# Score products of a two-block transformer kernel, all contracted over 96 or 128 rows

## The chip, the cores and the metric

The kernel runs on one core of a Trainium2 chip. The metric is the device time of one execution in microseconds (us); lower is better. TensorE (PE) does the matrix products, its weight loads have a row of their own in the profile (PEld), VectorE (DVE), ScalarE (ACT) and GpSimd (POOL) do the elementwise work, and DMA transfers are issued from SyncE's queue (SP) and from POOL's.

## The reference, cut to what matters

Two blocks of two layers each work on 512 tokens of width 1024, everything in float32. In the first block each of 8 query heads of 64 columns, sharing 2 key heads, attends to 256 context tokens and to a window around its own 128 tokens; the context's queries attend to the context alone:

```python
s_loc = jnp.einsum('bqkgd,bnkd->bkgqn', qi, ks).astype(jnp.float32)
s_ctx = jnp.einsum('bqkgd,bnkd->bkgqn', qi, kc).astype(jnp.float32)
p = sink_softmax(jnp.concatenate([s_ctx, s_loc], axis=-1), sink_b).astype(v.dtype)
```

The second block has 16 heads of three kinds: 6 of kind A (mixtures of dilated windows, 64 columns), 4 of kind B (the difference of two softmaxes, each over 32 columns), and 6 of kind C (latent, 64 + 32 columns). All of them are causal:

```python
a = probs(q1, k1) - lam * probs(q2, k2)          # kind B
s = jnp.einsum('bqhd,bkhd->bhqk', qs, k)         # kind C
```

Both blocks go on with an output projection and norms, the second also with a gated feed-forward of width 2816. A modulation of the first block's layers comes from two vectors c and c_ctx.

## The kernel before

Every float32 operand of a large product is held as the sum of a high and a low part of a narrower kind (fp32r). `split` (line 175) makes them: `hi` on ACT writes the high part, `lo` on DVE subtracts it. `mm3` (line 208) then adds three products: high by high, high by low, low by high. Weights arrive on SP's queue in chunks of 512 KB and are split the same way (`w`, line 179).

The program is written as a sequence of steps. A scheduler orders them by their place in the text and by what they wait for, within the limits of the named buffers, and each engine then works through its own fixed queue. `high_priority(offset=n)` moves what stands inside ahead by n instructions. PSUM, where products land, is divided into three buffers `acc`, two score buffers `s` (`sps`), two for transposes (`tp`) and one for attention outputs (`pv`).

*First block's attention* (`first_mix`, `first_att`). The keys of both heads lie in KS as their high part, on both halves of the 128 rows, and in KTl as their low part, on the 64 rows of their own head. The queries Q hold the high part on 64 rows and the low part on the other 64. So one product over 128 rows (lines 819 and 825) gives high by high and low by high at once, and one over 64 rows (lines 820 and 826) adds high by low:

```python
nc.tensor.matmul(p1[:, kc], Q[:, g, hq, :], KS[:, g, kc], start=True, stop=False)
nc.tensor.matmul(p1[:, kc], Q[r, g, hq, :], KTl[r, kc], start=False, stop=True)
```

Between them stand the products of the next queries, of transposes and values, and of gate blocks (`tblock`). Layer 0 has 6 query tiles of 128 tokens (2 of them context), layer 1 has 4.

*Second block's attention* (`second_mix`, `att2`). Heads come in pairs, in the order of UNITS (line 34), here A B C B C A C A. `proj(i + 1)` projects the next pair's queries, keys and values (`proj_t`, 24 products of 512 columns each for kinds A and B) and splits them; then `att` of pair i follows, moved ahead by AHEAD = 102 instructions. `direct` (line 1113) leaves a pair of kind A or B in four tiles of 128 rows, qh, ql, kh, kl (`pair`, 8 buffers of the tag qk, line 1005); a head of kind A is 64 rows of them, one softmax of kind B 32 rows. `att2` makes three products for each of 4 query tiles:

```python
for k, (x, y) in enumerate(((0, 2), (0, 3), (1, 2))):
    for ps, s in zip(pss, subs):
        nc.tensor.matmul(ps[:, :w], s[x][:, tok], s[y][:, :w], start=(k == 0), stop=(k == 2))
```

The four tiles have w = 256, 256, 384 and 512 columns. For kind B, `subs` holds both softmaxes, so their products alternate. Line 1025 (DVE) then adds the distance table T, which POOL's queue loads for each head (line 947, two buffers), and takes the extreme; line 1029 (ACT) takes the exponential; line 1048 or 1050 (DVE) divides or combines; line 1060 transposes, lines 1063 to 1069 split, lines 1074 to 1077 multiply by the values. Kind C has queries and keys of 128 rows of its own and the same three products. `fin` of kind B norms the pair's output with a tile sq, kind C's projection uses a tile qu, and `vpair` a tile vt.

*Modulation* (`mod_rows`, `mod_later`). A product gives rows of which four are used, copied by line 324 into a tile of 5 rows; line 369 contracts over these 4 rows, line 395 over 5.

## Time and profile before

| | us |
|---|---|
| median of 3 runs | 2070.19 (2068.41 to 2079.08) |
| span of the profiled execution, first to last instruction | 2059.4 |
| PE busy in it | 2006.9 (97%) |
| DVE busy | 1204.4 (58%) |
| ACT busy | 877.2 (43%) |
| POOL busy | 123.1 (6%) |

The profiled execution has no time of its own beside its span; between the span and the median of the runs lie 10.8 us. The granted TensorE clock is 0.993 of full speed on average. An instruction's row gives its engine, the line of the kernel, the tiles that it writes and reads, and its shape: `64*128 64x256` is a product that contracts 64 rows, with 128 columns of weights and 256 columns streamed. Products are pipelined, so that one starts before the end of the one before it; the distance from start to start is what one costs. Idle time stands in brackets with what ended it.

### The profile page before, as it was taken

Reading aid. Unit: us, or ns where it says so; the run is one execution under the profiler, and the core shown is the slowest. Engines: PE = TensorE matmul, PEld = TensorE weight load, DVE = VectorE, ACT = ScalarE, POOL = GpSimd, SP = SyncE. Lnnn points to the kernel's source line nnn. Section 1 sums busy time; section 2 is a strip of 40 time slices with the busy share of each in tenths; the row PEclk is TensorE's granted clock in tenths of the full one; section 3 lists DMA queues with packets and bytes.
Section 4 is the critical chain, followed back from the end, with each engine's and each line's share of the span. In section 5 each row is a group of like instructions: output and inputs, shape, how many; then the busy total and the mean of one; then the engine's idle time right before and its main releaser. Section 6 shows DMA issues by size and latency. Waiting matters only on the chain. (4 is left out here: it accounts for less than half of the span.)

```text
span 2059.4 us, 25829 instructions
## 1 busy us (share of the span) xinstructions
PE 2006.9 (97%) x9692; PEld 1584.7 (77%) x9692; DVE 1204.4 (58%) x2386; ACT 877.2 (43%) x1708; POOL 123.1 (6%) x230
## 2 busy tenths in 40 slices
PE   6999999999999999999999999999999999999997
PEld 4877778778776786767788888888677788888886
DVE  3758875366787575777643333346677664333434
ACT  4736553376455444656332222214566523222220
POOL 2000000021000020000100000011000010000001
PEclk9999999999999999999999999999999999999999
DMA  8413433134331163212342323316112333332321
GB/s 287 149 37 93 123 103 93 42 103 127 93 92 51 52 184 88 56 47 83 103 133 82 107 88 100 101 61 162 46 47 62 118 103 113 92 98 76 113 82 41
DMA packets 220448, 197.19 MB, mean 96 GB/s; under 512 B 30154, under 2 KB 178128, under 8 KB 220324
## 3 DMA queue, kind: packets, MB, share of 16 engines
q1 hardware_dynamic: 209940, 160.32, 26.8%
q0 software_dynamic: 10384, 35.24, 5.0%
q8 instruction: 76, 1.25, 0.3%
q14 instruction: 48, 0.39, 0.1%
HBM read 187.09 MB, written 12.03 MB: 97 GB/s over the span
## 5 line engine op out<-in xcount | busy, mean ns | idle before, releaser
L165 ACT ACTIVATE wh<-wr 128x1024 fp32r<-128x1024 f32 (+3 forms) x299 | 311.6, 1044 | 645.0 <-PE acc L213 304.6
L169 DVE TENSOR_TENSOR wl<-wr,wh 128x1024 fp32r<-128x1024 f32 (+3 forms) x299 | 358.5, 1202 | 268.6 <-ACT wh L165 267.8
L212 PE MATMUL acc<-xt,wh 128*128 128x512 f32 (+1 forms) x1200 | 470.3, 392 | 0.0
L213 PE MATMUL acc<-xt,wh 128*128 128x512 f32 (+1 forms) x1200 | 469.1, 391 | 0.0
L214 PE MATMUL acc<-xt,wl 128*128 128x512 f32 (+1 forms) x1200 | 468.3, 390 | 0.0
L213 PEld LDWEIGHTS acc<-xt,wh 128*128 128x128 f32 x1200 | 227.2, 189 | 47.1 <-issue 3.8
L212 PEld LDWEIGHTS acc<-xt,wh 128*128 128x128 f32 x1200 | 226.6, 189 | 47.4 <-issue 3.2
L214 PEld LDWEIGHTS acc<-xt,wl 128*128 128x128 f32 x1200 | 226.7, 189 | 45.1 <-issue 1.8
L212 PE MATMUL acc<-wh,ht 128*128 128x512 f32 (+1 forms) x494 | 192.6, 390 | 0.0
L213 PE MATMUL acc<-wl,ht 128*128 128x512 f32 (+1 forms) x494 | 191.9, 388 | 0.0
L214 PE MATMUL acc<-wh,ht 128*128 128x512 f32 (+1 forms) x494 | 191.5, 388 | 0.0
L165 ACT ACTIVATE pth<-tps 128x384 fp32r<-128x384 f32 (+1 forms) x176 | 90.9, 537 | 101.0 <-PE tps L789 50.6
L169 DVE TENSOR_TENSOR ptl<-tps,pth 128x384 fp32r<-128x384 f32 (+1 forms) x176 | 105.0, 614 | 43.5 <-ACT pth L165 39.7
L1029 ACT ACTIVATE L<-L,nm 128x128 f32<-128x128 f32 (+3 forms) x160 | 89.2, 558 | 49.2 <-DVE nm L1025 47.7
L214 PEld LDWEIGHTS acc<-wh,ht 128*128 128x128 f32 x494 | 92.8, 188 | 21.6 <-DVE ht L169 0.9
L212 PEld LDWEIGHTS acc<-wh,ht 128*128 128x128 f32 x494 | 92.8, 188 | 20.6
L213 PEld LDWEIGHTS acc<-wl,ht 128*128 128x128 f32 x494 | 92.8, 188 | 20.1
L1025 DVE CUSTOM_DVE_ANT_0 L<-sps,T 128x128 f32<-128x128 f32 (+3 forms) x160 | 76.3, 487 | 46.9 <-PE sps L1022 45.7
L1400 DVE SCALAR_TENSOR_TENSOR h<-h,acc 128x512 f32<-128x512 f32 (+1 forms) x50 | 33.2, 665 | 114.6 <-PE acc L214 114.6
L1366 DVE SCALAR_TENSOR_TENSOR th<-th,acc 128x512 f32<-128x512 f32 x42 | 28.9, 688 | 112.1 <-PE acc L214 111.9
L214 PE MATMUL acc<-wh,xt 128*128 128x256 f32 (+2 forms) x256 | 85.5, 335 | 1.1 <-DVE xt L169 0.8
L212 PE MATMUL acc<-wh,xt 128*128 128x256 f32 (+2 forms) x256 | 85.2, 334 | 0.1
(309 smaller groups left out, 3265.9 us busy)
## 6 DMA issues: line engine op xcount, KB each, us to landing
wr<-in_w_in_dram SPq DMA_DIRECT2D x66, 512.0 KB, 4.1
wr<-in_w_gate_dram SPq DMA_DIRECT2D x44, 512.0 KB, 3.9
wr<-in_w_up_dram SPq DMA_DIRECT2D x44, 512.0 KB, 3.9
wr<-in_w_down_dram SPq DMA_DIRECT2D x42, 512.0 KB, 3.6
wr<-in_w_mod_dram SPq DMA_DIRECT2D x40, 512.0 KB, 4.4
wr<-in_w_o_dram SPq DMA_DIRECT2D x32, 256.0 KB, 3.0
T<-skew POOLq DMA_DIRECT2D x26, 256.0 KB, 3.0
x<-in_x_dram POOLq DMA_DIRECT2D x8, 512.0 KB, 7.0
```

What stands on the lines that cost most here:

```text
L165: self.nc.scalar.activation(out, in_, AF.Copy, scale=scale)
L169: self.nc.vector.tensor_tensor(out, in_, hi.bitcast(F32), op=ALU.subtract)
L212: mm(ps, lh, rh, start=(first and i == 0), stop=False)
L213: mm(ps, lh, rl, start=False, stop=False)
L214: mm(ps, ll, rh, start=False, stop=(last and i == n - 1))
L1025: nc.vector.tensor_tensor_reduce(lc, ps[:, :n], T[:, SEQ - n : SEQ], 1.0, 3.0e38, op0=ALU.add, op1=ALU.min, accum_out=nm[:, i : i + 1],)
L1029: nc.scalar.activation(lc, lc, AF.Exp, bias=nm[:, i : i + 1], scale=-1.0, accum_out=sums[:, i : i + 1])
L1366: nc.vector.scalar_tensor_tensor(th, th, 0.5, pu, op0=ALU.mult, op1=ALU.mult)
L1400: nc.vector.scalar_tensor_tensor(h[:, c], h[:, c], ALPHA if gi == 0 else 1.0, ps, op0=ALU.mult, op1=ALU.add)
```

## The change

The rows that a score product contracts become 128 everywhere, or 96 for three of the four sub-heads of a pair of kind B:

- First block: KTl becomes KL, a tile with both heads side by side, low parts on the head's own 64 rows and zeros (two POOL memsets) on the others; lines 820 and 826 contract over all 128 rows of Q and KL. KL lies in the layer's pool, and the convolution's tile `cv` takes buffers of the tag rp8 to make room.
- Kind A: for each head, Q holds the high part on its 64 rows and the low part on the other 64, K the high part on both halves (POOL copies it), L the low part beside zeros (POOL memset). Two products, Q by K and Q by L, take the place of three.
- Kind B: for each softmax, three strips of 32 rows hold high, low and high of the queries against high, high and low of the keys (the second high is copied by POOL), so one product takes the place of three. The fourth softmax's strips begin at row 32, and row strip 0 holds zeros there.
- Kind C keeps its three products.
- Query buffers (tag qk) become 12 in place of 8; vt gets 2 buffers, which qu and sq share.
- UNITS becomes B C B C A C A A.
- `att2` takes each softmax's products as a list and makes them one softmax after the other.
- Modulation rows are tiles of 128 rows, the selector is padded with zeros, and lines 369 and 395 contract over 128.

```diff
-UNITS = (("A", 0, 0), ("B", 0, 3), ("C", 0, 5), ("B", 1, 4), ("C", 1, 6), ("A", 1, 1), ("C", 2, 7), ("A", 2, 2))
+UNITS = (("B", 0, 3), ("C", 0, 5), ("B", 1, 4), ("C", 1, 6), ("A", 0, 0), ("C", 2, 7), ("A", 1, 1), ("A", 2, 2))
...
-        self.sel = self.fp.tile([5, 4], F32, name="sel")
-        nc.gpsimd.dma_start(self.sel, A["sel"])
+        self.sel = self.fp.tile([P, 4], F32, name="sel")
+        nc.gpsimd.memset(self.sel, 0.0)
+        nc.gpsimd.dma_start(self.sel[0:5], A["sel"])
...
-        r = self.fp.tile([5, 512], F32, tag=tag, bufs=bufs, name="mrow")
-        nc.scalar.copy(r[0:4], ps[0:4])
+        r = self.fp.tile([P, 512], F32, tag=tag, bufs=bufs, name="mrow")
+        nc.scalar.copy(r, ps)
...
-                    mc[:, 2 * b : 2 * b + 2], r[0:4, b * P : (b + 1) * P], self.sel[0:4, 0:2], start=True, stop=True
+                    mc[:, 2 * b : 2 * b + 2], r[:, b * P : (b + 1) * P], self.sel[:, 0:2], start=True, stop=True
...
-        KTl = self.fp.tile([P, CTX + SEQ], F32R, tag="ktl", bufs=1, name="ktl")
+        KL = pool.tile([P, 2, CTX + SEQ], F32R, tag="ktl", bufs=1, name="ktl")
+        for g in range(2):
+            nc.gpsimd.memset(KL[64 - g * 64 : 128 - g * 64, g].bitcast(F32), 0.0)
...
-                self.lo(KTl[r, kc], tp[r, 0:P], KS[r, g, kc])
+                self.lo(KL[r, g, kc], tp[r, 0:P], KS[r, g, kc])
...
-                tt = pool.tile([P, SEQ + 2], F32, tag="cv", bufs=2, name="cv")[:, : n + 2]
+                tt = pool.tile([P, SEQ + 2], F32, tag="rp8", bufs=3, name="cv")[:, : n + 2]
...
-                nc.tensor.matmul(p1[:, kc], Q[r, g, hq, :], KTl[r, kc], start=False, stop=True)
+                nc.tensor.matmul(p1[:, kc], Q[:, g, hq, :], KL[:, g, kc], start=False, stop=True)
...
-                    nc.tensor.matmul(p2[:, :nl], Q[r, g, hq, :], KTl[r, kl], start=False, stop=True)
+                    nc.tensor.matmul(p2[:, :nl], Q[:, g, hq, :], KL[:, g, kl], start=False, stop=True)
...
-        vt = pool.tile([P, SEQ], F32, tag="vt", bufs=1, name="vt")
+        vt = pool.tile([P, SEQ], F32, tag="vt", bufs=2, name="vt")
...
-    def pair(self, pool):
-        return tuple(pool.tile([P, SEQ], F32R, tag="qk", bufs=8, name="qk") for _ in range(2))
+    def qk(self, pool, n=2):
+        return tuple(pool.tile([P, SEQ], F32R, tag="qk", bufs=12, name="qk") for _ in range(n))
...
-            for k, (x, y) in enumerate(((0, 2), (0, 3), (1, 2))):
-                for ps, s in zip(pss, subs):
-                    nc.tensor.matmul(ps[:, :w], s[x][:, tok], s[y][:, :w], start=(k == 0), stop=(k == 2))
+            for ps, s in zip(pss, subs):
+                for k, (x, y) in enumerate(s):
+                    nc.tensor.matmul(ps[:, :w], x[:, tok], y[:, :w], start=(k == 0), stop=(k == len(s) - 1))
...
-        def direct(cq, ck, cv, scale):
-            qh, ql = self.pair(pool)
-            self.split(qh, ql, self.proj_t(W, cq), scale=scale)
-            kh, kl = self.pair(pool)
-            self.split(kh, kl, self.proj_t(W, ck))
-            return qh, ql, kh, kl, self.vpair(pool, self.proj_t(W, cv))
-
         def dilated(p, o):
-            qh, ql, kh, kl, V = direct(p * P, 384 + p * P, 768 + p * P, -0.125)
+            Q, K, L = self.qk(pool), self.qk(pool), self.qk(pool)
+            ps = self.proj_t(W, p * P)
+            for j in range(2):
+                r, ro = (slice(x * 64, x * 64 + 64) for x in (j, 1 - j))
+                self.split(Q[j][r], Q[j][ro], ps[r], -0.125)
+            ps = self.proj_t(W, 384 + p * P)
+            for j in range(2):
+                r, ro = (slice(x * 64, x * 64 + 64) for x in (j, 1 - j))
+                nc.gpsimd.memset(L[j][ro].bitcast(F32), 0.0)
+                self.split(K[j][r], L[j][r], ps[r])
+                nc.gpsimd.tensor_copy(K[j][ro], K[j][r])
+            V = self.vpair(pool, self.proj_t(W, 768 + p * P))
...
-                    yield self.att2(t2, [(qh[r], ql[r], kh[r], kl[r])], T, V, j, o)
+                    yield self.att2(t2, [[(Q[j], K[j]), (Q[j], L[j])]], T, V, j, o)
...
         def differential(p, o):
-            b = 1152 + p * P
-            qh, ql, kh, kl, V = direct(b, b + 256, b + 512, -(32.0 ** -0.5))
+
+            b0 = 1152 + p * P
+            QK = []
+            for c, scale in ((b0, -(32.0 ** -0.5)), (b0 + 256, None)):
+                ps = self.proj_t(W, c)
+                tiles = self.qk(pool, 4)
+                for b, t in enumerate(tiles):
+                    x, y = [i for i in range(b == 3, 3 + (b == 3)) if i != b]
+                    r, rx, ry = (slice(i * 32, i * 32 + 32) for i in (b, x, y))
+                    if b == 3:
+                        nc.gpsimd.memset(t[0:32].bitcast(F32), 0.0)
+                    low, dup = (rx, ry) if scale else (ry, rx)
+                    self.split(t[r], t[low], ps[r], scale)
+                    nc.gpsimd.tensor_copy(t[dup], t[r])
+                QK.append([t if b == 3 else t[0:96] for b, t in enumerate(tiles)])
+            V = self.vpair(pool, self.proj_t(W, b0 + 512))
...
-                    subs = []
-                    for s in range(2):
-                        r = slice(j * 64 + s * 32, j * 64 + s * 32 + 32)
-                        subs.append((qh[r], ql[r], kh[r], kl[r]))
+                    subs = [[(QK[0][i], QK[1][i])] for i in (2 * j, 2 * j + 1)]
...
-                    yield self.att2(t2, [qs[j] + (kh, kl)], Tc, V, j, o)
+                    qh, ql = qs[j]
+                    yield self.att2(t2, [[(qh, kh), (qh, kl), (ql, kh)]], Tc, V, j, o)
```

## Rows read from the trace of the kernel before

**Rows 1.** The page's first part: busy us, share of the span, instructions

```profile
PE 2006.9 (97%) x9692; PEld 1584.7 (77%) x9692; DVE 1204.4 (58%) x2386; ACT 877.2 (43%) x1708; POOL 123.1 (6%) x230
```

**Rows 2.** Busy time by stretch: us, PE, PEld, DVE, ACT, POOL, clock, DMA share, GB/s

```profile
126.00:336.00 210.00, 208.70 (x1040) 156.41 (x1039) 168.05 (x401) 116.56 (x225) 2.73 (x8) 1.00 0.33 90
336.00:400.00 64.00, 62.74 (x327) 52.23 (x326) 25.85 (x39) 17.79 (x30) 0.51 (x1) 0.97 0.23 68
524.00:688.00 164.00, 163.43 (x729) 116.90 (x729) 127.56 (x290) 86.84 (x158) 1.63 (x3) 1.00 0.31 84
...
783.00:982.00 199.00, 193.52 (x943) 137.95 (x942) 144.50 (x378) 123.09 (x301) 12.54 (x20) 0.99 0.22 63
```

**Rows 3.** PE in order of time, kind C's products: start us, us, instruction

```profile
856.94 0.87 PE L1022 MATMUL sps<-kb,qk 128*128 128x512 f32 x3
857.65 0.40 PE L212 MATMUL acc<-xt,wh 128*128 128x512 f32 x1
```

**Rows 4.** PE in order of time, first block's attention

```profile
130.17 0.40 PE L213 MATMUL acc<-wl,xt 128*128 128x512 f32 x1
130.40 0.28 PE L819 MATMUL sps<-kth,q 128*128 128x256 f32 x1
130.61 0.38 PE L820 MATMUL sps<-ktl,q 64*128 64x256 f32 x1
130.92 0.50 PE L214 MATMUL acc<-wh,xt 128*128 128x512 f32 x1
131.26 0.39 PE L212 MATMUL acc<-wh,xt 128*128 128x512 f32 x1
131.49 0.40 PE L213 MATMUL acc<-wl,xt 128*128 128x512 f32 x1
```

**Rows 5.** Lines 820 and 826: count, ns min/median/max, first and last start, forms

```profile
L820 PE MATMUL sps<-ktl,q x80: 378/381/386, 128.9 to 672.5; 64*128 64x256 f32 x80
...
L826 PE MATMUL sps<-ktl,q x64: 379/409/443, 164.1 to 674.1; 64*128 64x256 f32 x32, 64*128 64x384 f32 x32
```

**Rows 6.** Line 1022, kinds A and B together; kind A's first and last run

```profile
L1022 PE MATMUL sps<-qk x336: 271/381/578, 783.4 to 1617.7; 32*128 32x256 f32 x48, 64*128 64x256 f32 x36, 64*128 64x384 f32 x24, 32*128 32x384 f32 x24
...
783.40 0.74 PE L1022 MATMUL sps<-qk 64*128 64x256 f32 x4
...
1617.12 0.97 PE L1022 MATMUL sps<-qk 64*128 64x512 f32 x3
```

**Rows 7.** PE in order of time, kind B's products: first run, a run of six

```profile
808.44 0.38 PE L1022 MATMUL sps<-qk 32*128 32x256 f32 x1
...
811.44 0.62 PE L1022 MATMUL sps<-qk 32*128 32x256 f32 x6
812.00 0.51 PE L214 MATMUL acc<-xt,wl 128*128 128x512 f32 x1
```

**Rows 8.** Splits of 128 and of 64 rows: count, ns min/median/max

```profile
L165 ACT ACTIVATE qk<-acc x20: 577/595/600, 772.5 to 1608.4; 128x512 fp32r<-128x512 f32 x20
...
L169 DVE TENSOR_TENSOR qk<-acc,qk x10: 683/692/693, 779.2 to 1609.1; 128x512 fp32r<-128x512 f32 x10
...
L171 DVE SCALAR_TENSOR_TENSOR q<-tps,q x20: 683/688/697, 127.8 to 623.0; 64x512 fp32r<-64x512 f32 x20
```

**Rows 9.** POOL's instructions: count, busy us, mean ns, idle before, releaser

```profile
L219 POOL TENSOR_SCALAR rv<-bna 128x1 f32<-128x1 f32 x16 | 18.9, 1183 | 787.5 <-DVE bna L1295 787.5
...
L219 POOL TENSOR_SCALAR rv<-ss 128x1 f32<-128x1 f32 x12 | 2.3, 194 | 36.8 <-ACT xs L425 36.7
...
L700 POOL MEMSET G<- 128x512 f32 x4 | 2.0, 530 | 0.0
...
L288 POOL TENSOR_SCALAR nsink<-nsink 128x16 f32<-128x16 f32 x1 | 0.3, 268 | 4.2 <-DMA nsink<-in_sink_dram 4.2
```

**Rows 10.** Line 369: all of them, and the first run of eight

```profile
L369 PE MATMUL acc<-sel,mrow x64: 246/246/267, 24.6 to 319.5; 4*128 4x2 f32 x64
...
24.63 1.05 PE L369 MATMUL acc<-sel,mrow 4*128 4x2 f32 x8 [0.66 <-ACT mrow L324]
```

More of the change, by code (lines that the diff above doesn't have):

```diff
@@ L382, in mod_gate @@
             gp = self.row(self.fp, self.A["g_post"][l][hh * 512 : hh * 512 + 512], "mrow", 1, 5)
-            nc.vector.scalar_tensor_tensor(r, r, 0.5, gp, op0=ALU.mult, op1=ALU.mult)
+            nc.vector.scalar_tensor_tensor(r[0:5], r[0:5], 0.5, gp, op0=ALU.mult, op1=ALU.mult)
             res.append(r)
@@ L394, in gate_rows @@
                 ps = self.acc()
-                nc.tensor.matmul(ps, self.sel[:, 2 + s : 3 + s].to_broadcast([5, P]), gs[hh], start=True, stop=True)
+                nc.tensor.matmul(ps, self.sel[:, 2 + s : 3 + s].to_broadcast([P, P]), gs[hh], start=True, stop=True)
                 nc.scalar.copy(r[:, hh * 512 : hh * 512 + 512], ps)
@@ L617, in attend @@
                 self.lo(Q[ro, g], tv[r], Q[r, g], -0.125)
-            for f in self.first_att(l, ap, gt, isc, t, Q, KS, KTl, Vs, hT):
+            for f in self.first_att(l, ap, gt, isc, t, Q, KS, KL, Vs, hT):
                 todo.append(f)
@@ L765, in fourier, with first_att @@
             mix(*f)
-    def first_att(self, l, pool, gt, isc, t, Q, KS, KTl, Vs, hT):
+    def first_att(self, l, pool, gt, isc, t, Q, KS, KL, Vs, hT):
         nc = self.nc
@@ L1123, in att @@
             def att():
                 for j in range(2):
-                    r = slice(j * 64, j * 64 + 64)
                     T = self.table(t2, 2 * p + j)
-                    yield self.att2(t2, [(qh[r], ql[r], kh[r], kl[r])], T, V, j, o)
+                    yield self.att2(t2, [[(Q[j], K[j]), (Q[j], L[j])]], T, V, j, o)
             return att, None
         def differential(p, o):
-            b = 1152 + p * P
-            qh, ql, kh, kl, V = direct(b, b + 256, b + 512, -(32.0 ** -0.5))
+            b0 = 1152 + p * P
@@ L1138, in att @@
                     T = self.table(t2, 6 + 2 * p + j)
-                    subs = []
-                    for s in range(2):
-                        r = slice(j * 64 + s * 32, j * 64 + s * 32 + 32)
-                        subs.append((qh[r], ql[r], kh[r], kl[r]))
+                    subs = [[(QK[0][i], QK[1][i])] for i in (2 * j, 2 * j + 1)]
                     yield self.att2(t2, subs, T, V, j, o, nlam=nlam, inv=inv[:, j:8:2])
             def fin():
-                sq = t2.tile([P, SEQ], F32, tag="sq", bufs=1, name="sq")
+                sq = pool.tile([P, SEQ], F32, tag="vt", bufs=2, name="sq")
                 nc.scalar.activation(sq, o, AF.Square)
@@ L1182, in latent @@
                 self.mm3(ps, [(uq[k][0][:, h, :], uq[k][1][:, h, :], cT[k][0], cT[k][1]) for k in range(2)])
-                u = t2.tile([P, SEQ], F32, tag="qu", bufs=2, name="qu")
+                u = pool.tile([P, SEQ], F32, tag="vt", bufs=2, name="qu")
                 nc.vector.tensor_tensor(u, ps, self.rope2, op=ALU.mult)
-                qh, ql = self.pair(pool)
+                qh, ql = self.qk(pool)
                 self.split(qh, ql, u)
```

## The prediction

> **What bounds the kernel now.** I read the page's busy times first: TensorE (PE) is busy 97% of the span [rows 1], so nothing gets faster unless PE's queue does. Next the stretches of the two attentions [rows 2]: in the first block's (126 to 336 and 524 to 688 us) PE is busy 99%, VectorE (DVE) 80% and 78%; in the second block's (783 to 982, and an equal one 650 us later) PE 97%, DVE 73%, ScalarE (ACT) 62%. Busy does not mean working, though, so the third view is PE's own order in time.
>
> There the start-to-start step is the price of a product. Three 512-column products that contract 128 rows take 0.71 us to the next start, 0.237 each [rows 3], so 256 columns should take 0.118 and the mean score product of the second block (256, 256, 384, 512 columns: 352) 0.163. Around a 64-row product the steps are longer [rows 4]: into it 0.21 instead of 0.118, out of it 0.31 instead of 0.118, and the 512-column product behind it needs 0.34 instead of 0.237 to the next. From 130.17 to 131.49 are 1.32 us; three 512s and two 256s at their plain price are 0.95. **One return from 128 rows to 64 and back costs 0.37 us**, more than the product itself. That time is booked as PE busy, which is why no idle row shows it.
>
> **The change, part by part.**
>
> *First block, zeros beside the low parts.* All 144 products with the low keys (L820, L826) contract 64 rows [rows 5], each between 128-row ones. With KL they contract 128 rows: same count, same columns. The gain is the return: between 0.19 (the step out of 64 rows alone) and 0.37 each; I take 0.37, because all three longer steps stand in one uninterrupted row. 144 x 0.37 = **53 us of PE** (lower end 27). DVE and ACT do the same splits as before. The zeros cost four memsets of 64x768 on POOL, about 0.8 us each by 0.53 for 512 columns [rows 9], at the head of a layer, hidden behind the key projections; without that cover 3 us in all.
>
> *Second block, kind A.* Per head and query tile two products instead of three: 6 heads x 4 tiles x 2 layers = 48 fewer, 48 x 0.163 = 7.8 us. The 144 products of now stand in 68 runs, from the first at 783.40 to the last at 1617.12 [rows 6]; 68 x 0.37 = 25. Together **33 us** (lower end 7.8 + 68 x 0.19 = 21).
>
> *Kind B.* One product instead of three: 192 become 64 (A's and B's are the 336 of [rows 6]), 128 x 0.163 = 21 us; these too stand in 68 runs, the first at 808.44 [rows 7], 25 us. But the 32-row products of the two softmaxes partly overlap: six of 256 columns take 0.56 us to the next start [rows 7], not 0.71. With 16 such runs that takes off 2: **44 us** (lower end, with 0.19 a return, 32). The Trainium skill, "TensorE: Matmul & The Clock Gate", Part 3 (Packing small matmuls), speaks against this edit: products in distinct 32-row groups run concurrently, so stacking gives the overlap up. By it alone six would cost three, 192 products 15.6 us instead of 31, and B's gain would be 30. The row shows a small part of that overlap, so I keep 44.
>
> *Modulation.* 64 four-row products (L369) in runs of eight become 128-row ones; 8 x 0.37 = 3 us [rows 10], part of it while the first loads arrive. I count 2. The wider sel and copies cost columns, not rows, so nothing.
>
> PE sum: 53 + 33 + 44 + 2 = **132 us of 2059**.
>
> *What it adds.* A pair of kind A needs 4 splits into high and low parts where it had 2, a pair of kind B 8 where it had 2. That is 3 x 2 + 2 x 6 = 18 more ACT and 18 more DVE instructions a layer. A piece of 64 rows takes as long as one of 128, 688 against 692 ns on DVE, 595 on ACT [rows 8]: +12.4 us DVE and +10.7 us ACT a layer. POOL gets 22 copies a layer (2 per A pair, 8 per B pair) and 10 memsets. No copy stands in the trace: between 0.53 us (a memset of as many columns) and 2.7 (194 ns for one column, 268 for 16, carried on to 512) [rows 9]. I take 0.8, nearest to the memset, which also runs through 512 columns. 18 us a layer on an engine that is busy 12.5 of 199 us [rows 2]. POOL's queue also issues the distance tables (L947); a copy can stand behind a table load that waits for its buffer, but the pair it serves comes one pair later, some 25 us (199 / 8). So nothing, as long as a B pair's 8 copies stay under that; the largest bound, 8 x 2.7 = 22, still does. Copies may also hold DVE up: if a third of 18 us collided, 6 us a layer.
>
> *Moves at no cost.* Unit order: B now opens, its projections run before 783 us under the latent projections, and C pairs still have another pair between them. Twelve query buffers hold two neighbouring pairs (8 + 4, 6 + 6) as eight did with four each. The shared vt and rp8 buffers wait at worst for a transpose of the same pair. SP's queue carries the same weights in the same number, the w_o blocks in the new order. Cover gone, the opening B pair would wait for its copies, 8 x 0.8 = 6 us a layer.
>
> **What is late next.** DVE. A second attention would need 199 - 38.5 = 160 us of PE and 144.5 + 12.4 = 157 of DVE; the first ones 180 and 141 of PE against 168 and 128 of DVE. Two engines equally loaded, passing tiles back and forth through two score buffers, don't both reach 100%. I let each stage end where DVE is at 90%: 174 us, 25 saved, twice; 187 us, 23 saved; 142 us, 22 saved. With the 2 of modulation 97 us. The profiled execution's span is 2059.4, 10.8 under the median of the runs shown, and I leave that distance: 2070 - 97 = **1973 us**.
>
> **Rivals.**
> - *PE stays the bound* (0.2). The stretch behind the first attention has DVE at 26 of 64 us [rows 2]; gate blocks pulled forward would fill PE's gaps. Against it: DVE at 95% or more. Full 132 us: 1938.
> - *96 rows still drain* (0.1). No product of that height stands in the trace; if PE treats it as it does 32 and 64, B's 64 products keep returns of 0.37, 24 us. PE then needs 172 us a stage, near DVE's 174: about 1990 with the stalls of both.
> - *The chain already sets the attentions* (0.06). If DVE at 73 to 80% is all that the two score buffers allow, PE's time turns into idle time and only modulation gains: 2066. Against it, PE is busy 97 to 99% there [rows 2], so it is DVE that waits for PE and not the other way.
> - *The returns are not the rows* (0.05). If the long steps came from the operands and not the height, only columns go: 29 us less 9 for the splits, 2050. C's 128-row products, of the same line and buffers, have plain steps [rows 3], which speaks against it.
> - *POOL starves PE* (0.04), the slower side. The same kind of one-column POOL operation takes 194 ns in one place and 1183 in another, where DVE runs the long layer-norm operations [rows 9]. The Trainium skill, "SBUF — State Buffer" (Who interferes with whom), names a port pair that DVE operations with two SBUF inputs and POOL reads lock against each other; this agrees with that row. If copies stretch as far (0.8 x 6 = 5 us), 8 of them take 40 us, 15 more than the pair's lead; four B pairs make 60, which the gain still covers. It decides from 8 x c - 25 = 97 / 4 on, c = 6.2 us; at 9 us (a stretched bound between the two) 4 x 47 = 188 us, so 2070 - 97 + 188 = 2161.
>
> **How the numbers follow.** My forecast has 0.55. Faster by over 0.5% (10 us, about what a measurement of this kernel can tell from no change) holds in the first three cases and the fourth rival: 0.90. Within: 0.06. Slower: 0.04. The range goes from 1932, just under the full gain, to DVE at 84%, some 50 us saved, 2020; this leaves out the 0.15 of the last three rivals.
>
> **What would show it.** Right: L820 and L826 as 128-row products with steps of 0.118 and 0.16; 336 L1022 products of kinds A and B become 160; PE busy near 1875 us (2007 - 132), DVE 25 us more, POOL some 35 more; each second attention 174 us long with DVE near 90% and PE idle behind DVE's scores or splits. Wrong: 96-row products with steps of 0.3 into and out of them; PE idle behind a POOL copy; attention stages as long as now with PE at 80%.

## The result, and the profile after

The changed kernel takes **2002.94 us** (median of 4 runs, 2000.64 to 2007.32) against 2069.3 of the kernel before (4 runs, 2057.85 to 2079.08). The ratio is 0.970 with an interval of 0.9672 to 0.9727. The forecast was 1973 in a range of 1932 to 2020: the sign and the range held, the gain is 66 us where 97 were forecast. The profiled execution took 2004.78 us, its span is 2003.0, so 56.4 of the gain can be followed from span to span. The other ten lie in the runs of before, which spread over 21 us; beside the experiments the kernel before took 2063 to 2065 us in the median, and the gain against those is 61.

The page's head, busy times and granted clock in 40 slices (a digit is tenths of full speed):

```profile
span 2003.0 us, 25662 instructions
...
PE 1918.2 (96%) x9516; PEld 1571.8 (78%) x9516; DVE 1224.4 (61%) x2422; ACT 895.0 (45%) x1744; POOL 171.3 (9%) x299
...
PEclk9999999999999999999999999999889999999999
```

Against [rows 1], PE is busy 88.7 us less and the span is only 56.4 shorter, so PE now stands idle 32 us more than before. DVE gained 20 us, POOL 48.

By stages, the first attentions counted from the first product of scores to the first of the output projection, the second ones from the last product of the stage ahead to the first with w_o, all by PE's order in time (the last column belongs to an experiment below, the changed kernel with the old UNITS):

| stage | before, us | after, us | saved | forecast | saved, old order |
|---|---|---|---|---|---|
| first block's attention, layer 0 | 261.7 | 235.3 | 26.4 | 23 | 26.6 |
| first block's attention, layer 1 | 170.3 | 148.2 | 22.1 | 22 | 22.1 |
| second block's attention, layer 0 | 235.4 | 231.3 | 4.1 | 25 | 13.8 |
| second block's attention, layer 1 | 236.3 | 234.0 | 2.3 | 25 | 12.6 |
| all the rest | 1155.7 | 1154.2 | 1.5 | 2 | 1.1 |

The first block did what was forecast, and a little more. Its two attentions after the change (us, PE, PEld, DVE, ACT, POOL, clock, DMA share, GB/s):

```profile
126.00:297.00 171.00, 167.47 (x969) 141.06 (x968) 155.78 (x380) 111.16 (x216) 3.85 (x13) 1.00 0.37 105
498.00:636.00 138.00, 136.85 (x709) 110.34 (x709) 122.42 (x286) 85.50 (x157) 1.81 (x7) 1.00 0.35 92
```

DVE is busy 91 and 89% there, and PE still 98 and 99%. Nearly all of the gain forecast for the second block is missing, and that is the question of the experiments.

**Where the first block's gain is seen.** PE in order of time at the first scores of the changed kernel:

```profile
127.59 0.28 PE L822 MATMUL sps<-kth,q 128*128 128x256 f32 x1
127.71 0.28 PE L823 MATMUL sps<-ktl,q 128*128 128x256 f32 x1
127.83 0.29 PE L822 MATMUL sps<-kth,q 128*128 128x256 f32 x1
127.95 0.28 PE L823 MATMUL sps<-ktl,q 128*128 128x256 f32 x1
128.07 0.39 PE L212 MATMUL acc<-wh,xt 128*128 128x512 f32 x1
...
744.07 0.28 PE L1025 MATMUL sps<-qk 96*128 96x256 f32 x1
744.19 0.40 PE L214 MATMUL acc<-ct,wl 128*128 128x512 f32 x1
744.43 0.28 PE L1025 MATMUL sps<-qk 96*128 96x256 f32 x1
744.55 0.40 PE L212 MATMUL acc<-ct,wh 128*128 128x512 f32 x1
```

Every step is 0.12 us for 256 columns and 0.24 for 512. The 0.21, 0.31 and 0.34 of [rows 4] are gone. The same holds for the 96-row products of kind B (744.07 and after): the 512 columns ahead of one go on after 0.24 us, and the 96-row product itself after 0.12. So 96 rows cost no return, and that rival falls.

**Where the second block's gain went.** Busy time by stretch, in the same columns; the two second attentions of the kernel before first:

```profile
745.00:981.00 236.00, 230.35 (x1131) 171.44 (x1130) 166.66 (x430) 138.23 (x334) 19.26 (x35) 0.99 0.30 83
1397.00:1633.00 236.00, 230.66 (x1127) 171.60 (x1126) 167.16 (x429) 138.53 (x333) 18.11 (x34) 0.99 0.29 81
```

The same two stretches of the kernel after, and three pieces of the first:

```profile
695.00:926.00 231.00, 211.24 (x1039) 167.62 (x1037) 179.37 (x446) 147.55 (x351) 43.01 (x71) 0.94 0.33 93
1342.00:1576.00 234.00, 214.52 (x1040) 171.42 (x1038) 180.91 (x447) 148.14 (x350) 42.42 (x70) 0.93 0.31 91
...
735.00:755.00 20.00, 16.93 (x63) 12.20 (x64) 15.26 (x44) 12.32 (x33) 2.42 (x4) 0.74 0.24 66
...
780.00:790.00 10.00, 6.84 (x28) 4.39 (x26) 9.76 (x32) 8.73 (x25) 1.68 (x3) 0.92 0.32 83
790.00:800.00 10.00, 9.27 (x47) 7.47 (x45) 5.89 (x19) 5.13 (x15) 0.00 (x0) 0.74 0.28 77
```

Three things are to be read here. PE is busy 91 and 92%, not 98: it stands idle about 20 us a stage, where it was 5.5. DVE is busy 78 and 77%, far from the 90% at which the forecast let the stage end; it is full only in bursts (9.76 of 10 us at 780) and half empty right after. And the mean granted clock fell from 0.99 to 0.94 and 0.93. The clock has two levels here, 1.2 and 2.4 GHz, so 0.94 of 231 us means 0.06 / 0.5 x 231 = 28 us at the lower one, and in the second stage 33; before it was some 5 and 5.

What that looks like instruction by instruction, PE of the kernel after at the opening of the stage (the bracket is idle time before, and what ended it):

```profile
735.26 0.66 PE L999 MATMUL acc<-ident,vt 128*128 128x128 f32 x4 [1.27 <-ACT vt L996]
736.81 1.77 PE L1261 MATMUL tps<-ident,xs 128*128 128x128 f32 x8 [0.89 <-DVE ct L171]
...
742.37 0.63 PE L213 MATMUL acc<-ct,wh 128*128 128x512 f32 x1
742.80 0.63 PE L214 MATMUL acc<-ct,wl 128*128 128x512 f32 x1
743.23 0.63 PE L212 MATMUL acc<-ct,wh 128*128 128x512 f32 x1
```

PE waited 1.27 us for the values' copy (vt) and 0.89 for a latent split (ct); then 512 columns take steps of 0.43 us, the lower clock, against 0.24 above. So a short hole can cost twice: once by itself, and again in the slow products behind it. Who makes the holes, by the waits of PE from 695 to 926 us (us in total, times, longest):

```profile
PE acc L999 <- ACT vt L996: 5.0, 4, 2.3
PE sps L1025 <- DVE nm L1028: 2.9, 6, 0.9
PE tps L1167 <- ACT sq L1164: 1.7, 1, 1.7
PE pv L1079 <- DVE V L1004: 1.5, 1, 1.5
...
PE sps L1025 <- POOL qk L1127: 0.8, 1, 0.8
```

And of DVE in the same stretch:

```profile
DVE L L1028 <- PE sps L1025: 11.9, 16, 2.7
DVE ptl L169 <- ACT pth L165: 8.4, 13, 1.5
DVE heads L1090 <- ACT heads L1089: 5.2, 7, 1.6
```

PE waits for ACT and DVE, and once for a copy of POOL; DVE waits for PE and ACT. No engine is the bound by its amount; each is late for another in turn.

### The profile page after: what moved, and what is told of

It reads as the page before. It is cut to its first block, busy times and chain, and to the rows that moved or that the text cites. A ratio compares the mean times of both kernels' runs of the same rounds, so it can differ in the third digit from the quotient of the medians.

```text
span 2003.0 us, 25662 instructions
## 1 busy us (share of the span) xinstructions
PE 1918.2 (96%) x9516; PEld 1571.8 (78%) x9516; DVE 1224.4 (61%) x2422; ACT 895.0 (45%) x1744; POOL 171.3 (9%) x299
## 4 chain that ended last, share of the span: by engine, by line
PE 81%; DVE 5%; ACT 5%; issue 2%; DMA 1%; POOL 1%; POOLq 0%; DVEq 0%; ACTq 0%; SPq 0%
PE acc L212 22%; PE acc L213 22%; PE acc L214 22%; PE sps L1025 2%; PE tps L1063 2%; PE tps L792 1%; PE pv L1079 1%; PE pv L803 1%; DVE wl L169 1%; ACT wh L165 1%; ACT L L1032 1%; PE pv L804 1%; PE pv L1080 1%; PE tps L410 1%; DMA wr<-in_w_mod_dram 1%
## 5 line engine op out<-in xcount | busy, mean ns | idle before, releaser
L212 PE MATMUL acc<-xt,wh 128*128 128x512 f32 (+1 forms) x1200 | 464.4, 387 | 1.2 <-DVE kb L169 0.7
L213 PE MATMUL acc<-xt,wh 128*128 128x512 f32 (+1 forms) x1200 | 463.0, 386 | 0.0
L1032 ACT ACTIVATE L<-L,nm 128x384 f32<-128x384 f32 (+3 forms) x160 | 88.9, 557 | 24.1 <-DVE nm L1028 23.5
L1028 DVE CUSTOM_DVE_ANT_0 L<-sps,T 128x512 f32<-128x512 f32 (+3 forms) x160 | 74.9, 486 | 26.1 <-PE sps L1025 24.7
L219 POOL TENSOR_SCALAR rv<-bna 128x1 f32<-128x1 f32 x16 | 18.8, 1173 | 792.0 <-DVE bna L1313 792.0
L214 PE MATMUL acc<-wh,xt 128*128 128x256 f32 (+2 forms) x256 | 84.9, 332 | 1.1 <-DVE xt L169 0.8
```

The lines of the kernel that those rows point to most:

```text
L212: mm(ps, lh, rh, start=(first and i == 0), stop=False)
L213: mm(ps, lh, rl, start=False, stop=False)
L214: mm(ps, ll, rh, start=False, stop=(last and i == n - 1))
L1028: nc.vector.tensor_tensor_reduce(lc, ps[:, :n], T[:, SEQ - n : SEQ], 1.0, 3.0e38, op0=ALU.add, op1=ALU.min, accum_out=nm[:, i : i + 1],)
L1032: nc.scalar.activation(lc, lc, AF.Exp, bias=nm[:, i : i + 1], scale=-1.0, accum_out=sums[:, i : i + 1])
```

## The experiments

The theory on the way in: the first block gives its 48 us, the second block's PE time is saved as well, but turns into idle time and lower clock. The rivals: the new order of pairs costs time by itself; DVE's added splits set the stage; POOL's copies do.

### The two halves apart

The first kernel has the first block's and the modulation's part of the change alone (the second block as before); the second has the second block's part alone, new order included.

The core of e1_first against the kernel after:

```diff
-UNITS = (("B", 0, 3), ("C", 0, 5), ("B", 1, 4), ("C", 1, 6), ("A", 0, 0), ("C", 2, 7), ("A", 1, 1), ("A", 2, 2))
+UNITS = (("A", 0, 0), ("B", 0, 3), ("C", 0, 5), ("B", 1, 4), ("C", 1, 6), ("A", 1, 1), ("C", 2, 7), ("A", 2, 2))
...
-            for ps, s in zip(pss, subs):
-                for k, (x, y) in enumerate(s):
-                    nc.tensor.matmul(ps[:, :w], x[:, tok], y[:, :w], start=(k == 0), stop=(k == len(s) - 1))
+            for k, (x, y) in enumerate(((0, 2), (0, 3), (1, 2))):
+                for ps, s in zip(pss, subs):
+                    nc.tensor.matmul(ps[:, :w], s[x][:, tok], s[y][:, :w], start=(k == 0), stop=(k == 2))
```

The core of e2_second against the kernel after:

```diff
-        r = self.fp.tile([P, 512], F32, tag=tag, bufs=bufs, name="mrow")
-        nc.scalar.copy(r, ps)
+        r = self.fp.tile([5, 512], F32, tag=tag, bufs=bufs, name="mrow")
+        nc.scalar.copy(r[0:4], ps[0:4])
...
-                nc.tensor.matmul(p1[:, kc], Q[:, g, hq, :], KL[:, g, kc], start=False, stop=True)
+                nc.tensor.matmul(p1[:, kc], Q[r, g, hq, :], KTl[r, kc], start=False, stop=True)
```

> The first block's part of the change and the modulation alone; the second block with its pair order, buffers and products as before. Theory: nearly all of the measured gain (66 us) comes from here, since the changed kernel's stages from the first score to the output projection are 26 and 22 us shorter in layers 0 and 1 and the second attention only 2 us a layer: 2069 - 50 = 2019 us (2013 to 2026). Rival: the second block's part also brings its share, a third or more of the 66 us, and this one alone 2030 us or more.

> The second block's part alone (pair order, 12 query buffers, kinds A and B stacked), first block and modulation as before. Theory: PE's relief turns into idle time and a lower granted clock, so 2055 to 2066 us, PE idle 15 us or more in each second attention. Rival (the sum of the terms as forecast): 50 us faster, 2020 us. Rival (the extra splits and copies cost more than the products give): 2072 us or more.

Measured: e1_first 2011.88 us, 0.9757 [0.973, 0.9784]; e2_second 2055.45, 0.9957 [0.9942, 0.9971]; before 2064.28 in both. The parts are 52.4 and 8.8 us and add up to the 61 of the whole; in each case the theory is nearer than its rivals, though e1_first gained more than its range allowed. The first block's part with the modulation's was forecast at 47. So 144 returns at 0.37 us, read from one uninterrupted row [rows 4], price it well. The second block's part is worth a sixth of the 50 forecast.

### The order alone, and each kind alone

e3_order is the kernel before with the new UNITS, and nothing else. e4_kind_b is the kernel after with kind A back at three 64-row products, e5_kind_a the kernel after with kind B back at three 32-row ones; both keep the new order.

e3_order against the kernel before:

```diff
-UNITS = (("A", 0, 0), ("B", 0, 3), ("C", 0, 5), ("B", 1, 4), ("C", 1, 6), ("A", 1, 1), ("C", 2, 7), ("A", 2, 2))
+UNITS = (("B", 0, 3), ("C", 0, 5), ("B", 1, 4), ("C", 1, 6), ("A", 0, 0), ("C", 2, 7), ("A", 1, 1), ("A", 2, 2))
```

The core of e4_kind_b against the kernel after:

```diff
-                    yield self.att2(t2, [[(Q[j], K[j]), (Q[j], L[j])]], T, V, j, o)
+                    yield self.att2(t2, [[(qh[r], kh[r]), (qh[r], kl[r]), (ql[r], kh[r])]], T, V, j, o)
```

The core of e5_kind_a against the kernel after:

```diff
-                    subs = [[(QK[0][i], QK[1][i])] for i in (2 * j, 2 * j + 1)]
+                    subs = []
+                    for s in range(2):
+                        r = slice(j * 64 + s * 32, j * 64 + s * 32 + 32)
+                        subs.append([(qh[r], kh[r]), (qh[r], kl[r]), (ql[r], kh[r])])
```

> The kernel before with the new pair order B C B C A C A A alone; eight buffers hold it. Theory: the order by itself changes little, 2063 to 2077 us. Rival: the order puts kind B's attention beside the small projections of kind C in the first half of the stage and costs what the products gain: 2085 us or more.

> The changed kernel with kind A back at three products over 64 rows from four tiles (two splits, no copies); kind B stacked. PE gets 33 us of returns and products back. Theory: A's phases have PE to spare only in part, so 2003 to 2020 us. If PE's idle time in the second attention takes it all up: within 5 us of 2003. If A's products carried PE's path: 2030 us or more.

> The changed kernel with kind B back at three products over 32 rows from four tiles (two splits, no copies); kind A stacked, new order. Theory (B's stacking costs on DVE, ACT and POOL what it gives on PE; the first runs put it at 9 us the worse): 1990 to 2003 us. Rival (as forecast, B's stacking is worth 44 us of PE): 2025 us or more.

Measured: e3_order 2085.04 us, 1.0102 [1.0083, 1.0122]: **the order alone costs 21 us**, against the theory. e4_kind_b 2043.76, 0.9893 [0.9872, 0.9914], over the 2030 us of the case in which A's products carry PE's path; e5_kind_a 2003.96, 0.9696 [0.9664, 0.9727], against the rival. In the new order, then, kind A's stacking is worth 0.9893 - 0.970, some 40 us, and kind B's nothing that can be told from the spread of e5_kind_a's own runs (1995.55 to 2008.62). The second attentions of e3_order:

```profile
749.00:995.00 246.00, 239.70 (x1128) 174.02 (x1127) 166.25 (x429) 137.68 (x333) 19.02 (x35) 0.97 0.28 79
1411.00:1660.00 249.00, 243.41 (x1127) 176.98 (x1125) 167.23 (x429) 137.83 (x332) 18.05 (x34) 0.95 0.27 77
```

The same instructions as before on every engine, and PE needs 22 us more for them. In PE's order kind A's 64-row products now stand in 84 runs instead of 68, so 16 more returns, 16 x 0.37 = 6 us; and the clock is at 1.2 GHz for 0.03 / 0.5 x 246 + 0.05 / 0.5 x 249 = 40 us, 30 more than before, which takes 15. The two give 21. The forecast had put the order under "moves at no cost".

The lower clock here does not come from more holes: PE stands idle 12 us in the two stages of e3_order, and 11 in those of the kernel before. Where it fell for longest, PE had no idle time at all (busy time by stretch, e3_order):

```profile
930.00:941.00 11.00, 11.00 (x48) 7.30 (x46) 6.99 (x17) 6.20 (x13) 0.63 (x1) 1.00 0.24 73
941.00:955.00 14.00, 14.00 (x30) 7.90 (x30) 4.66 (x14) 3.39 (x10) 0.54 (x1) 0.51 0.21 57
```

From 937.67 to 941.42 us six of kind A's 64-row products stand there one by one between 128-row products, each with its return. A return is booked as busy, so a busy PE is no sign that its clock will stay up.

What the lower clock costs can be read from e5_kind_a alone: its run with a mean granted clock of 0.993 took 1995.55 us, the one with 0.986 took 2008.62. That is 0.007 / 0.5 x 2000 = 28 us more at the lower level, and 13 us more in all, about half.

### The change in the old order

e8_kind_a_old is e5_kind_a, e9_after_old the whole change, both with the UNITS of before.

```diff
-UNITS = (("B", 0, 3), ("C", 0, 5), ("B", 1, 4), ("C", 1, 6), ("A", 0, 0), ("C", 2, 7), ("A", 1, 1), ("A", 2, 2))
+UNITS = (("A", 0, 0), ("B", 0, 3), ("C", 0, 5), ("B", 1, 4), ("C", 1, 6), ("A", 1, 1), ("C", 2, 7), ("A", 2, 2))
```

> As the one before, kind A stacked and kind B not, but with the pair order of before (A B C B C A C A). Theory (the order alone cost 21 us and keeps costing): 1970 to 1985 us. Rival (the order cost only as long as A's products drained PE; A's stacking repaid just that): within 6 us of the new order's version.

> The changed kernel with nothing but the pair order put back to A B C B C A C A. Theory (order costs 20 us by itself): 1978 to 1992 us. Rival (with both kinds stacked the order is worth nothing): 1997 to 2009 us. Rival (an A pair's six and a B pair's eight buffers do not fit into twelve at once, and the second pair's splits wait): 2012 us or more.

Measured: e8_kind_a_old 1995.13 us, 0.9657 [0.964, 0.9675]; **e9_after_old 1985.41**, 0.961 [0.9591, 0.9628]. One line put back makes the changed kernel 17 us faster, as the theory had it; it beats both kernels. Here kind B's stacking is worth 10 us (1995.13 to 1985.41). e8_kind_a_old came out as neither forecast: with kind A alone stacked the order is worth 9 us (2003.96 to 1995.13). The second attentions of e8_kind_a_old:

```profile
695.00:921.00 226.00, 216.42 (x1106) 167.23 (x1104) 169.90 (x435) 141.98 (x339) 29.09 (x51) 0.99 0.33 96
1337.00:1567.00 230.00, 221.53 (x1104) 171.64 (x1102) 171.29 (x435) 142.42 (x338) 28.05 (x50) 0.96 0.32 92
```

And those of e9_after_old, with the opening that was shown of the kernel after:

```profile
695.00:917.00 222.00, 203.58 (x1042) 162.62 (x1040) 178.43 (x447) 147.35 (x351) 43.09 (x71) 0.98 0.34 97
1333.00:1557.00 224.00, 206.34 (x1042) 165.90 (x1040) 179.44 (x448) 147.97 (x351) 41.67 (x70) 0.97 0.33 95
...
735.00:755.00 20.00, 19.51 (x96) 15.07 (x95) 16.30 (x39) 14.12 (x33) 6.30 (x10) 1.00 0.34 93
```

Between e9_after_old and the kernel after PE is busy 15.8 us longer in the two stages (425.8 against 409.9) with the same products, and idle only about 3 more. At the lower clock stand 22 us there and 61 here; half of the difference is 20, enough for it. So what the new order costs the changed kernel is mostly clock: from 735 to 755 us PE has 96 instructions and a clock of 1.00 in the old order, 63 and 0.74 in the new. It is so in every run: all four of e9_after_old had a mean clock of 0.992, those of the kernel after 0.980 to 0.983, which is 36 to 48 us more at the lower level. The holes themselves hardly differ, 36 us in the old order and 39 in the new, so it is not their sum that brings the clock down.

PE's saving by kinds can be read from the same rows. From before to e8_kind_a_old PE is busy 23.1 us less (461.0 to 438.0), with some 14 us more at the lower clock, so 30 at an equal clock for kind A: 33 were forecast. From there to e9_after_old it is 28.0 for kind B at an equal clock, where 44 were forecast; in the new order, from e5_kind_a (PE 228.7 and 219.9 us busy, clock 0.94 and 0.98) to the kernel after, it is some 34.

Part of what is missing was in the forecast's own row [rows 7]. It took six products at 0.56 us to the next start as a small overlap, and a full return of 0.37 beside it. But the 0.56 already holds the long step out of the run. The wider products of kind B in the kernel before show how large the overlap is:

```profile
815.59 1.21 PE L1022 MATMUL sps<-qk 32*128 32x512 f32 x6
816.73 0.47 PE L1060 MATMUL tps<-ident,L 128*128 128x128 f32 x1
```

Six products of 512 columns take 1.14 us to the next start, step out included. Their plain price is 1.42, that of three 0.71. Seven of the sixteen runs of six stand undisturbed at the full clock; with the steps into and behind them they cost 0.06 us less than their plain price in the mean, where the forecast reckons 0.22 more. Over all runs this brings the 44 to about 40. The Trainium skill, "TensorE: Matmul & The Clock Gate", Part 3 (Packing small matmuls), has products in distinct 32-row groups run concurrently. The trace agrees where the two softmaxes' products alternate: the six at 811.44 us start in three pairs, 5 to 10 ns apart. The prediction's 30, worked out by that part of the Trainium skill, let all 192 overlap; half of them stand in runs of one to four products, where little of it shows.

Of the 12 us from 40 to 28, some 7 are ends of products: 512 columns are booked as 0.40 us busy, where the next start follows after 0.24, so each product in front of a hole adds to PE's busy time, and e9_after_old has 38 such holes more than e8_kind_a_old in the two stages. The last 5 stay open.

### Is PE still the bound?

e6_thrice issues the first product of each list of kinds A and B three times, in the kernel after; e11_old_thrice does so in e9_after_old. These are 224 products more, 224 x 0.163 = 36 us of PE's time at the full clock; each overwrites the one before.

```diff
                 for k, (x, y) in enumerate(s):
+                    if k == 0 and len(s) < 3:
+                        for _ in range(2):
+                            nc.tensor.matmul(ps[:, :w], x[:, tok], y[:, :w], start=True, stop=True)
```

> The changed kernel with the first product of every score of kinds A and B issued three times (the first two are overwritten): 112 x 2 products of 0.163 us, 36 us more PE work in the second attentions. Theory (PE is not what bounds them): under 18 us slower, less idle time on PE. If PE bounds them: 36 us slower. If the lower granted clock there is what costs: faster or the same, with the clock in the two stages above 0.95 instead of 0.93 and 0.91.

> The changed kernel with the pair order of before, and the first product of every score of kinds A and B issued three times, 36 us more PE work. With the new order the same edit made it 10 us faster. Theory (that gain was the granted clock: 61 us at the lower level became 14; with the old order only 20 us are at the lower level, so there is little to win): 1984 to 2000 us. Rival (extra products help for another reason, such as the order of the queues): 1970 to 1980 us.

Measured: e6_thrice 1992.73 us, 0.9644 [0.9627, 0.966], **ten us faster with 36 us more work** for PE; e11_old_thrice 1981.55, 0.9588 [0.9561, 0.9616], against 0.961 without the extra products, so the same or a little faster, between what theory and rival gave. The stages of e6_thrice, then those of e11_old_thrice:

```profile
694.00:922.00 228.00, 218.83 (x1153) 178.70 (x1151) 178.69 (x446) 148.64 (x351) 45.18 (x71) 0.99 0.32 95
1338.00:1565.00 227.00, 218.22 (x1152) 178.25 (x1150) 179.57 (x447) 148.84 (x350) 44.05 (x70) 0.98 0.33 94
...
693.00:916.00 223.00, 217.17 (x1157) 179.08 (x1155) 180.60 (x448) 148.42 (x352) 42.15 (x71) 0.99 0.34 98
1331.00:1553.00 222.00, 216.28 (x1155) 178.57 (x1154) 181.43 (x448) 148.70 (x350) 40.93 (x70) 0.99 0.34 96
```

The extra products went into the holes: in e6_thrice idle time fell from 39 us to 18 in the two stages, and the clock rose to 0.99 and 0.98 (14 us at the lower level, not 61). So the lower clock of the kernel after is a cost that filled holes give back. The old order shows the other point more cleanly, because there was little clock to win: in e11_old_thrice idle time fell from 36 us to 12, the clock can have given back some 7, and the stages are as long as without the extra products. PE is no longer the bound of these stages, for 36 us of work on it cost nothing.

### Does DVE's added work, or POOL, hold the stage?

e14_few_splits is e9_after_old with kind B's queries and keys split whole, two pairs of instructions where there were eight, without copies and memsets. It leaves out the stacking of kind B's strips, so that its four score products of a pair get other rows and the scores are other numbers; products, columns and rows are those of e9_after_old. A pair of kind B also takes four query buffers instead of eight.

```diff
-                tiles = self.qk(pool, 4)
-                for b, t in enumerate(tiles):
...
-                    self.split(t[r], t[low], ps[r], scale)
-                    nc.gpsimd.tensor_copy(t[dup], t[r])
...
+                t, u = self.qk(pool)
+                self.split(t, u, ps, scale)
+                QK.append([t[0:96], u[0:96], t[0:96], u])
```

> The changed kernel with the pair order of before, and kind B's queries and keys split by one pair of instructions over 128 rows each instead of four pairs over 32, with no copies and no zeros by POOL; the products keep their number, shape and order, but take whole tiles (this leaves out the stacking of kind B's strips, so B's scores are other numbers). Off come 12 ACT and 12 DVE instructions and 16 copies a layer. Theory (waits between the engines in their fixed order hold the stage, the added splits only in small part): 1975 to 1985 us against 1985 with the splits. Rival (DVE's added work is what eats PE's gain): 8.3 us a layer and more, 1960 to 1970 us. Rival (POOL's copies block DVE as well): under 1960 us.

Measured: 1970.92 us, 0.9548 [0.9532, 0.9564]; 0.961 less 0.9548 is 0.0062, 13 us, at the border between theory and rival. Its stages:

```profile
696.00:913.00 217.00, 202.79 (x1040) 164.70 (x1039) 169.11 (x434) 140.05 (x339) 29.35 (x51) 0.98 0.34 100
1329.00:1543.00 214.00, 199.22 (x1038) 161.80 (x1036) 170.06 (x435) 140.21 (x338) 28.11 (x50) 0.99 0.34 99
```

A layer has 9.3 us less of DVE, 7.5 less of ACT and 13.7 less of POOL (those of e9_after_old above), and is 6.4 us shorter. So what the run leaves out costs two thirds of its length on DVE, though DVE is busy under 80%. The run does not tell apart which of the three engines, or the buffers, gives it; some 3 of the 13 us may be clock (0.98 and 0.97 in e9_after_old).

e10_old_wpool gives POOL the low parts of every other weight chunk of the second attentions, in the old order, to relieve DVE.

```diff
-        self.split(h, l, raw)
+        self.hi(h, raw)
+        if self.wpool and self.wi % 2:
+            self.nc.gpsimd.tensor_tensor(l, raw, h.bitcast(F32), op=ALU.subtract)
+        else:
+            self.lo(l, raw, h)
```

> The changed kernel with the pair order of before, and every other low part of a weight chunk in the second block's mixing subtracted by POOL instead of DVE (same numbers). It takes about 10 operations of 1.2 us a layer from DVE. Theory (DVE's and ACT's chain, not their sum, holds the stage): 1978 to 1988 us. Rival (DVE's busy time bounds the stage): 1962 to 1975 us. Rival (POOL's reads of two SBUF operands block DVE or come late): 1992 us or more.

Measured: 2005.47 us, 0.9696 [0.9662, 0.9729], slower than e9_after_old by 0.0086 or 18 us, as the second rival had it. The two kinds of subtraction (count, busy us, mean ns, idle before):

```profile
L196 POOL TENSOR_TENSOR wl<-wr,wh 128x1024 fp32r<-128x1024 f32 x15 | 37.0, 2468 | 66.6 <-ACT wh L166 59.6 <-PE sps L1032 6.9
...
L170 DVE TENSOR_TENSOR wl<-wr,wh 128x1024 fp32r<-128x1024 f32 x265 | 324.0, 1224 | 250.4 <-ACT wh L166 246.7 <-PE tps L1268 2.8
```

One takes twice as long on POOL. In the first of the two stages score products now wait for key copies in POOL's queue behind them:

```profile
PE sps L1032 <- POOL qk L1134: 2.1, 2, 1.3
PE sps L1032 <- POOL qk L1158: 2.1, 2, 1.3
```

Nor was DVE relieved by as much as left it: 22 subtractions of some 1.2 us are 26 us, and its busy time fell by 7.5 (1222.2 to 1214.7). Some of its operations beside a subtraction on POOL took much longer than without; a copy of 128x96 took 2.15 us where it takes 0.20. POOL, then, has no room for such work. As the change uses it, PE waits for its copies 0.8 us a stage (1.7 in the old order); what they cost by way of DVE was not measured. The copies in the kernel after (count, busy us, mean ns, idle before):

```profile
L1151 POOL CAST qk<-qk 32x512 fp32r<-32x512 f32 x32 | 23.6, 738 | 49.0 <-ACT qk L165 48.7
...
L1127 POOL CAST qk<-qk 64x512 fp32r<-64x512 f32 x12 | 10.2, 851 | 106.4 <-ACT qk L165 105.7 <-PE acc L213 0.5
```

### What in the order costs

e12_order2 takes a third order, in which A opens the stage as before but the kinds go round A C B.

```diff
+UNITS = (("A", 0, 0), ("C", 0, 5), ("B", 0, 3), ("A", 1, 1), ("C", 1, 6), ("B", 1, 4), ("A", 2, 2), ("C", 2, 7))
```

> The changed kernel with a third order, A C B A C B A C: each B pair's attention stands beside an A pair's projections (72 products of 512 columns) and each C projection beside an A attention. Theory (PE falls idle where kind B's attention has only kind C's small projections beside it): shorter than with either order, 1965 to 1982 us, with less PE idle time and less time at the lower clock. Rival (what matters is that kind A opens the stage): 1980 to 1990 us. Rival (an A pair beside a B pair needs 14 query buffers of 12, and the wait costs): 1992 us or more.

Measured: 1986.06 us, 0.9609 [0.9577, 0.9642], the same as e9_after_old and against the theory. Spreading the B pairs further apart brought nothing, and the wait for buffers does not show; what the two good orders share is that A opens and no two A pairs stand side by side at the end. Which of these counts was not tried. Nor was a form of kind B with whole splits and keys beside zeros, which would keep its scores right without the sixteen small splits.

## Why the prediction was right and wrong

- *The returns.* Right in mechanism and size for the first block: 47 forecast with the modulation, 52.4 measured (e1_first). L820 and L826 are 128-row products with the steps forecast. The rivals "the returns are not the rows" and "96 rows still drain" fall with the steps shown above.
- *Kind A.* 33 forecast, about 30 of PE's time at an equal clock. *Kind B.* **Mis-sized**: 44 forecast, 28 measured in the old order and some 34 in the new. The row of six was read wrong: its 0.56 us hold the step out of the run, which the forecast added once more, and the overlap is larger than the small part that it saw.
- *"Moves at no cost. Unit order."* **This step failed.** The order costs 21 us in the kernel before (e3_order) and 17 in the changed one (e9_after_old). The forecast asked whether buffers and queues would cover the opening B pair's copies; what the order changed was the runs into which PE's products fall and the places at which the clock drops.
- *"I let each stage end where DVE is at 90%."* **This step failed too**, in the second block, by the same amount again. DVE reached 78% in the kernel after and 80% in e9_after_old. In the first block DVE went to 91 and 89% with PE still at 98 and 99%, and more was saved there than the rule allowed. The number, taken from no row, says little about a stage. Without the order's cost a second attention saves 13 us (last column of the first table), not 25.
- *The clock* was no term at all. In the kernel before it stood at 0.99 here [rows 2]. After the change it fell behind holes of PE, so a relief of PE can bring it down; but e9_after_old has nearly as many holes and little of it, and in e3_order it fell without any.
- *The added work.* DVE +20 us against 25, ACT +18 against 21, POOL's copies 0.74 and 0.85 us against 0.8. POOL as a whole gained 48 against some 35: the memsets of the second attentions had no price. The sizes hold in the main, but that the splits and copies would lie beside other work didn't: of kind B's, two thirds of their length on DVE show in the stage (e14_few_splits).
- *Rivals.* "PE stays the bound" falls with e11_old_thrice. "POOL starves PE" falls: PE waits 0.8 us a stage for POOL's copies. "The chain already sets the attentions" was wrong for the first block, and for the second it is nearest to what happened; its own terms give 2070 - 2 = 2068, not 2066.

That the range held is in part luck: the first block gave its forecast 47 and 5 more, and the second's 50 shrank to 9 for reasons that the forecast did not have.

The sum for the two second attentions: PE's relief at an equal clock was 30 + 28 = 58 us (77 forecast). In the old order 6 of it went to the clock and 25 to idle time (11 us before, 36 in e9_after_old), which leaves, with the rounding of the clock, the 26 of the first table. The new order took 16 more of PE's time and 3 of idle time, which leaves, with the rounding of the stretches, the 6 of the first table. That the order's 16 are clock rests on the granted clock of the rows and of every run, and on e6_thrice, which gave 10 back by filling holes; what about the order brings the clock down stays open.

## What to carry to other kernels

Count the returns between contraction heights in PE's order of time, not in the source: one cost 0.37 us here, booked as busy, and zeros or copies that fill the rows removed it. Where 32-row products of different strips stood in runs of six, their overlap paid for the return. When such an edit relieves an engine which was 98% busy, don't price the rest by the next engine's busy share; look for who waits for whom, and expect that PE's holes can cost again through the clock. And a new order of work is a change of its own: measure it alone before it travels with another.

## What the runs showed of the hardware that was not expected

Holes of about 1 us each (1.27 and 0.89 us at 735 us) went ahead of a stretch at 1.2 GHz, in which 512 columns take 0.43 us from start to start instead of 0.24. In e3_order the clock fell to 0.51 from 941 to 955 us with no hole ahead, among 64-row products. More products than needed made the kernel faster (e6_thrice, 36 us more work, 10 us less time). Kind B's 32-row products overlapped by more than one merged row lets one see: six of 512 columns took 1.14 us where three would take 0.71 and six in turn 1.42. And subtractions given to POOL stretched operations of DVE beside them, a copy from 0.20 to 2.15 us (e10_old_wpool).
